# Memory gates stored turned and loaded by transposing DMAs, and a new pacing of the weight sums, in a two-layer decoder trunk

## The chip, the cores and the metric

The kernel runs on one core of one Trainium2 chip. The metric is device time in microseconds (us) of one execution. TensorE (PE in the profile) does the matmuls, VectorE (DVE), ScalarE (ACT) and GpSimd (POOL) the elementwise work. DMAs are issued by SyncE (SP) and by POOL, each through a queue of its own, and share 16 DMA engines.

## The reference

Two layers are computed on a residual stream x of 512 rows by 2048 columns. Each layer projects x with one wide matrix into three groups of heads of 128 columns, each head with a gate path of its own:

```
A) forgetting attention: 6 heads, a log-forget bias, causal
B) sparse attention: 6 heads with rotary; an indexer picks the top 128 keys of each query
C) memory attention: 4 heads into 256 memory rows
y = concat(A, B, C) * silu(gate);  x <- LayerNorm(alpha*x + y @ w_out)
```

What matters here is the gate of group C: a matrix of 512 rows by 4 x 128 columns per layer. The kernel uses it turned, with the 128 columns of a head on the partitions and the 512 rows along them, as the attention output stands when the gate multiplies it.

## The kernel before, in words

**Products.** Every float32 operand is split into a high part that the matmul takes exactly (ACT writes it, `whi`, `xh`) and the rest (DVE writes it, `wlo`, `xl`); a product is three matmuls. A 512-column matmul follows the one before it by about 0.227 us. The weights stream from DRAM in chunks (`raw`, two halves of 128x1024), loaded by SP two chunks ahead (`load_w`, L355); each half is split by ACT and DVE a chunk and a half ahead of its matmuls (`split_w`, L421).

**Stages of a layer.** The tag `now` has the stage's name. "kv": the memory's keys and values. "index": the indexer's small products (chunks `small` and `iq`). "values": for six pairs of column blocks, the projections of values, gates, queries and keys, as seven Strassen-like products per pair (P1, P7, P2, Q6, Q4, then in the next stage Q5 and Q3), so that each column block j = 2 x pair or 2 x pair + 1 comes out as four tiles of 128 rows by 512 columns. "heads": the last two products Q5 and Q3 of all six pairs, with the attention of the 16 heads scheduled between their matmuls. "out": the output projection, again by such products, and then the norm and the next layer's operands (`next_x`, L1484), which run into the next layer's "kv".

**Sums of weights.** Some products need the sum of two weight blocks. Half of the pairs' sums are made ahead in DRAM (`weight_sums`, L556): POOL issues a copy of one block into a `sum` block (1 MB), and later a DMA that adds the other block. There are 44 such DMAs a layer. Each is preceded on POOL by `pool_waits` (L539): DVE (in "values" ACT) writes a small tile `mark`, and POOL waits for it with a multiply into `seen`, so that the sum goes out at that place of the program. `paced` (L573) sets how many ticks lie between two of them. In "kv" and "heads" none is issued. A layer's sums are begun at that layer's "index" stage; `all_sums` (L590) waits after layer 0's last one until layer 1 has begun. Layer 0's 44 sums and layer 1's 44 are otherwise alike. For the P7 product of pairs 1 to 5 no sum is made: the second block is loaded (`other`) and DVE adds it to `raw` (`pair_w`, L383).

**The column blocks' way to the heads.** A finished block is stored in DRAM by POOL and loaded again by SP, one head at a time. There are two ways. Blocks in `ROWS` (L98) are stored by rows as float32 (`store_v`, L1335; a Q5 or Q3 result is added to what is stored by an accumulating DMA) and loaded by head with a strided DMA (`load_head`, L1345, issued at L1349). The others are stored as 16-bit halves, rearranged by ACT (`halves`, L1353; `store_turned`, L1360), and loaded turned by a transposing DMA (`load_turned`, L1374, issued at L1378); a Q5 or Q3 result is added by DVE to what Q6 stored, which SP loads ahead of it (`load_base`, L1317, called at the end of the chunk before). Column block 7 holds the gates of the memory's four heads (`MEMG`), column block 11 those of the last four other heads. Both are in `BY_PE` (L97): they go by rows, and TensorE turns them, four transposes of 128x128 per head into a PSUM bank `gt` (`turned`, L706; `gate`, L716). Block 7 is finished in "heads" by pair 3's Q5 and Q3.

**Order.** "heads" and "out" order their steps with flows (`flow`, `advance`): generators that are stepped between matmuls when a clock modelled in the program says that an engine is free. So a step that becomes longer or falls away moves others. Tiles of 128x512 share a pool of 69 slots; a tile can be written when the slot's earlier tile has been read, by an engine or by a DMA. `store_x` (L1465) stores the next layer's residual (`x<-z`) by POOL; its slots are used again by the operands `xf`, `xh`, `xl` of `next_x`.

Of the kernel before, what the change touches and what calls it, by code (L numbers as in the profile page):

```python
# [23 lines left out]
DEPTH = 2  # L24
# [14 lines left out]
PACE = 2  # L39
# [54 lines left out]
MEMQ, MEMG = 5, 7  # L94
QK = {"f": (2, 4), "d": (6, 8)}
VALUES, GATES = (0, 1, 9), (10, 3, 11)
BY_PE = (7, 11)  # L97
ROWS = (*VALUES, *BY_PE)  # L98
IN_DRAM = 1
VAL_FIRST = (("P1", 0), ("P7", 0), ("P1", 1), ("P7", 1), ("P2", 0), ("Q6", 0), ("Q6", 1), ("P2", 1),  # L100
# [35 lines left out]
def stream():  # L136

    wall = all_chunks()
    where = {c: i for i, c in enumerate(wall)}
    out = []  # L140

    def product(kind, l, name, pair, gs=(0, 1)):
        right = PRODUCTS[name][2]
        for g in gs:
            at = lambda step: where[kind, l, 2 * pair + step[1], 2 * step[0] + g]
            if name in GROWN:
                of, step = GROWN[name]
                src = ("grown", (of, at(step)))
            elif kind == "val" and right == "T3" and pair >= IN_DRAM:
                src = ("pair", tuple(at(step) for step in PAIRED[right]))  # L150
            elif isinstance(right, str):
                src = ("sum", (kind, l, right, pair, g))
            else:
                src = ("wall", at(right))
            out.append(({"val": "vs"}.get(kind, kind), l, (name, pair), g, src))

    for i, c in enumerate(wall):
        kind, l, j = c[:3]
        if kind == "out":
            if c == ("out", l, 0, 0):  # L160
                for name, pair in OUT_ORDER:
                    product("out", l, name, pair)
        elif kind == "val":
            if c == ("val", l, 0, 0):
                early = [x for x in wall if x[1] == l and (x[0], x[2]) in HEAD_CHUNKS]
                for order in (VAL_FIRST, VAL_SECOND):
                    for pair in range(PAIRS):
                        for name, g in order:
                            product("val", l, name, pair, (g,))
                        if order is VAL_FIRST:  # L170
                            for _ in range(EARLY_AT[pair]):
                                x = early.pop(0)
                                out.append((*x, ("wall", where[x])))
        elif (kind, j) not in HEAD_CHUNKS:
            out.append((*c, ("wall", i)))
    return out
# [81 lines left out]
def kernel(  # L258
# [26 lines left out]
    def uid(name):  # L285
        count[0] += 1
        return f"{name}_{count[0]}"
# [16 lines left out]
    def bank(name):  # L304
        return psum.tile([P, 512], F32, tag="b", name=uid(name))
# [13 lines left out]
    def split_lo(src, hi, lo):  # L319
        nc.vector.tensor_tensor(lo, src, hi.bitcast(F32), op=ALU.subtract)  # L320
# [10 lines left out]
    chunks = stream()  # L331
# [85 lines left out]
    def last_half(i):  # L417

        return i >= len(chunks) - 4
# [119 lines left out]
    def pool_waits():  # L539

        mark, seen = small("mark", 1), small("seen", 1)
        if now[1] == "values":
            nc.scalar.activation(mark, mhalf, AF.Copy)
        else:
            nc.vector.tensor_copy(mark, mhalf)
        nc.gpsimd.tensor_tensor(seen, mark, mhalf, op=ALU.mult)
# [3 lines left out]
    def block(kind, l, pair, g, step):  # L550
        return wall[where[kind, l, 2 * pair + step[1], 2 * step[0] + g]]

    def add_weights(key, src):
        nc.gpsimd.dma_start(sums[key], src, accum_op=ALU.add, max_dma_last_dim=2 * DM)

    def weight_sums(kind, l, names, pairs, some=(0, 1)):  # L556

        for name in names:
            for n in some:
                step = SUM_STEPS[name][n]  # L560
                for pair in pairs:
                    for g in range(2):
                        key = (kind, l, name, pair, g)
                        src = block(kind, l, pair, g, step)
                        pool_waits()
                        if n:
                            add_weights(key, src)
                        else:
                            sums[key] = dram.tile([P, DM], F32, name=uid("sum"))
                            nc.gpsimd.dma_start(sums[key], src, max_dma_last_dim=2 * DM)  # L570
                        yield

    def paced(gen):  # L573

        n = 0
        for _ in gen:
            n += 1
            while now[1] in ("kv", "heads"):
                yield 1
            yield {"out": 3, "index": 1 + n % 2}.get(now[1], PACE)  # L580

    def value_sums(l):

        for n in range(2):
            yield from weight_sums("val", l, ("T3",), range(IN_DRAM), (n,))
        for pair in range(PAIRS):
            for n in range(2):
                yield from weight_sums("val", l, ("T1",), (pair,), (n,))

    def all_sums():  # L590


        for l in range(DEPTH):
            yield from paced(value_sums(l))
            yield from paced(weight_sums("out", l, ("T3", "T1"), range(2)))
            while l + 1 < DEPTH and now[0] == l:
                yield 1

    crow_d = [dram.tile([H_FOX, SEQ], F32, name=f"crow{l}") for l in range(DEPTH)]
# [11 lines left out]
    now = (0, "index")  # L611
# [51 lines left out]
    def free(n, eng):  # L663
        banks["held"] -= n
        freed.extend([clock.at[eng] + 0.1] * n)
# [22 lines left out]
    def drain(done):  # L688

        start = clock.at["PE"]  # L690
        while not done():
            advance()
            if not done():
                clock.at["PE"] += 0.2
            assert clock.at["PE"] < start + 100
# [17 lines left out]
    def fetch(key, j, c):  # L713
        return (load_head if j in BY_PE else load_turned)(key, j, c)

    def gate(key, of, there, j):  # L716

        if j in BY_PE:
            yield "PE", 1, there
# [8 lines left out]
        nc.vector.scalar_tensor_tensor(t, t, 1.0, g, op0=ALU.add, op1=ALU.mult)  # L728
        if j in BY_PE:
            free(1, "DVE")  # L730
# [31 lines left out]
    def mem_head(l, j):  # L762
# [3 lines left out]
        nc.sync.dma_start(km.bitcast(F32), km_d[l][j])  # L766
        if MEMQ in BY_PE:
            yield "PE", 1, there + 3
# [8 lines left out]
        split_lo(tp, *q)  # L777
        if MEMQ in BY_PE:
            free(1, "DVE")
# [403 lines left out]
    place_out = [0]  # L1183
# [254 lines left out]
    def load_res(l, st, dc):  # L1438
        z[st, dc] = slot("z")
        src = x_in if l == 0 else x1_d  # L1440
        nc.gpsimd.dma_start(z[st, dc], src[st * P:(st + 1) * P, dc * 512:(dc + 1) * 512])
# [169 lines left out]
    def ahead_of(i):  # L1611
        return i < len(chunks) and chunks[i][0] == "vs" and chunks[i][2][0] in ("Q5", "Q3")

    first = {l: min(i for i, c in enumerate(chunks) if c[1] == l) for l in range(DEPTH)}
    for i, (kind, l, j, col, _) in enumerate(chunks):
        late = last_half(i)
        if kind == "out":
            step = OUT_ORDER.index(j)
            name, pair = j
            if step == col == 0:  # L1620
                now, place_out[0] = (l, "out"), 0
            drain(lambda: (PRODUCTS[name][1], 2 * col + 1) in left)
            chain, aname, _, targets = PRODUCTS[name]
            opens = name in ("P1", "P2", "Q6")
            if col == 0:
                if opens:
                    chains[chain, pair] = [bank("z"), bank("z")]
                zs = chains[chain, pair]

                for st, dc in RES_LOADS.get(step, ()):  # L1630
                    load_res(l, st, dc)
                place_out[0] = step
        elif kind == "vs":
            name, pair = j
            aname = PRODUCTS[name][1]
            opens = name in VAL_OPENS
            if col == 0:
                if opens:
                    chains[VAL_CHAIN[name], pair] = [bank("v"), bank("v")]
            elif ahead_of(i + 1) and 2 * chunks[i + 1][2][1] + 1 not in ROWS:  # L1640
                load_base(*chunks[i + 1][2])
            zs = chains[VAL_CHAIN[name], pair]
        elif kind == "mv":
            if col == 0:
                out_ps = {m: bank("v") for m in range(2)}
        else:
            ps = bank("c")
        for h in range(2):
            n = 2 * i + h
# [27 lines left out]
            if kind == "out" and late:  # L1677
# [6 lines left out]
                if len(kept) == 16:  # L1684
# [3 lines left out]
                    for c in (0, 256):  # L1688
                        ps = bank("z")
                        c = slice(c, c + 256)  # L1690
# [21 lines left out]
            elif kind == "mv":  # L1712
                for m in range(2):
                    for nn in range(2):
                        k = 4 * col + 2 * h + nn
                        c = (k % 2) * 256 + m * P
# [3 lines left out]
            elif kind == "mk":  # L1720
                for kk in range(8):
                    k = 8 * h + kk
                    m = memT[k // 2]
                    c = (k % 2) * 256
# [59 lines left out]
        if kind == "mv" and l > 0:  # L1784
            now = (l, "kv")
        if kind == "small":
            now = (l, "index")
# [8 lines left out]
        if kind == "vs":  # L1796
            now = (l, "heads" if name in ("Q5", "Q3") else "values")
# [11 lines left out]
        if kind == "out" and step == col == 0:  # L1809
            now = (l, "out")  # L1810
# [100 lines left out]
```

## Time and profile before

| | us |
|---|---|
| median of 3 runs | 1887.84 |
| the runs | 1887.82 to 1891.09 |
| the profiled execution | 1887.66 |
| its span, first to last instruction | 1885.8 |
| around the span | 1.9 |
| mean granted TensorE clock | 0.995 |

The traced times are us from the span's start. Layer 0 ends and layer 1 begins at about 936; "heads" lies at about 535 to 810 in layer 0 and at about 1475 to 1750 in layer 1. PE's busy time is that of pipelined matmuls, so a full row says that PE was fed, not that it ran at its peak. A wait shows in PE's rows as a pair of brackets, with the time that PE was idle and what released it.

### The profile page before, as it was taken

What the parts mean: (1) busy time and instruction counts of PE and PEld (TensorE: products, weight loads), DVE (VectorE), ACT (ScalarE), POOL (GpSimd) and SP (SyncE); (2) the same over time, 40 slices, a digit from 0 to 9 for tenths busy, and PEclk for the clock granted to TensorE, in tenths of its full rate; (3) what the DMA queues carried; (4) which work ended last, traced back from release to release, by engine and by line L of the source; (5) the groups of instructions that cost most, each with busy time, mean ns of one, the idle gap of its engine ahead of it and who ended that gap; (6) DMA issues with size and microseconds to landing.
All of it is one profiled execution on the core that took longest, in us unless ns stands there. A gap on an engine that the chain in (4) does not pass through costs nothing.

```text
span 1885.8 us, 26424 instructions
## 1 busy us (share of the span) xinstructions
PE 1856.2 (98%) x8994; PEld 1576.5 (84%) x8994; DVE 1608.6 (85%) x2565; ACT 1079.9 (57%) x1752; POOL 410.1 (22%) x587
## 2 busy tenths in 40 slices
PE   9999999999999999999999999999999999999997
PEld 8998888887888888888899978888878888888886
DVE  6789789888789987889898998889787898878898
ACT  5776344444357887555476753454353578875553
POOL 0121222121233211240011221211221343113302
PEclk9999999999999999999999999999999999999999
DMA  9986998897999887986579969977979998879866
GB/s 351 294 239 162 300 303 241 298 273 267 251 244 286 257 220 206 265 210 215 190 256 282 264 173 307 324 235 272 290 266 237 248 299 234 220 215 269 239 215 142
DMA packets 230372, 474.20 MB, mean 251 GB/s; under 512 B 76368, under 2 KB 100944, under 8 KB 229980
## 3 DMA queue, kind: packets, MB, share of 16 engines
q1 hardware_dynamic: 176508, 300.48, 49.3%
q0 software_dynamic: 53152, 170.97, 35.5%
q8 instruction: 71, 1.16, 0.2%
q10 hardware_dynamic: 576, 1.05, 0.2%
q14 instruction: 65, 0.53, 0.1%
HBM read 402.15 MB, written 149.97 MB: 293 GB/s over the span
## 4 chain that ended last, share of the span: by engine, by line
PE 77%; DVE 9%; DMA 7%; ACT 3%; issue 2%; SPq 0%; POOL 0%; DVEq 0%; ACTq 0%; POOLq 0%
PE v L242 38%; PE c L242 17%; PE z L242 14%; DMA other<-in_wall_dram 4%; DVE wlo L242 4%; PE po L242 3%; PE ix L242 1%; PE s L242 1%; DMA grown<-sum 1%; PE pt L242 1%; ACT whi L242 1%; DVE raw L242 1%; DMA raw<-in_wall_dram 1%; DVE acc L242 1%; DVE rope L242 1%
## 5 line engine op out<-in xcount | busy, mean ns | idle before, releaser
L242 ACT ACTIVATE whi<-raw 128x1024 fp32r<-128x1024 f32 (+1 forms) x497 | 521.3, 1056 | 457.4 <-PE v L242 196.4
L242 DVE TENSOR_TENSOR wlo<-raw,whi 128x1024 fp32r<-128x1024 f32 (+1 forms) x497 | 601.7, 1217 | 133.0 <-ACT whi L242 130.5
L242 PE MATMUL v<-whi,vxh 128*128 128x512 f32 x768 | 306.7, 399 | 8.2 <-ACT whi L242 4.7
L242 PE MATMUL v<-wlo,vxh 128*128 128x512 f32 x768 | 302.0, 393 | 5.0 <-DVE wlo L242 5.0
L242 PE MATMUL v<-whi,vxl 128*128 128x512 f32 x768 | 301.4, 392 | 0.0
L242 PE MATMUL v<-whi,xh 128*128 128x512 f32 x576 | 224.4, 390 | 0.0
L242 PE MATMUL v<-wlo,xh 128*128 128x512 f32 x576 | 224.2, 389 | 0.0
L242 PE MATMUL v<-whi,xl 128*128 128x512 f32 x576 | 224.1, 389 | 0.0
L242 PE MATMUL c<-xh,whi 128*128 128x512 f32 (+1 forms) x544 | 197.9, 364 | 0.0
L242 PE MATMUL c<-xh,wlo 128*128 128x512 f32 (+1 forms) x544 | 197.8, 364 | 0.0
L242 PE MATMUL c<-xl,whi 128*128 128x512 f32 (+1 forms) x544 | 197.7, 363 | 0.0
L242 POOL TENSOR_TENSOR seen<-mark,mhalf 128x1 f32<-128x1 f32 x88 | 58.3, 662 | 635.6 <-ACT mark L242 452.6
L242 PEld LDWEIGHTS v<-whi,vxh 128*128 128x128 f32 x768 | 145.1, 189 | 40.2 <-ACT whi L242 7.4
L242 PEld LDWEIGHTS v<-wlo,vxh 128*128 128x128 f32 x768 | 145.3, 189 | 35.5 <-DVE wlo L242 8.5
L242 PEld LDWEIGHTS v<-whi,vxl 128*128 128x128 f32 x768 | 145.1, 189 | 30.8
L242 PE MATMUL z<-wlo,yh 128*128 128x512 f32 (+1 forms) x434 | 167.8, 387 | 2.0 <-DVE wlo L242 2.0
L242 PE MATMUL z<-whi,yh 128*128 128x512 f32 (+1 forms) x434 | 168.6, 389 | 0.0
L242 PE MATMUL z<-whi,yl 128*128 128x512 f32 (+1 forms) x434 | 167.7, 386 | 0.0
L242 PEld LDWEIGHTS v<-wlo,xh 128*128 128x128 f32 x576 | 108.3, 188 | 23.0 <-DVE wlo L242 0.3
L242 PEld LDWEIGHTS v<-whi,xh 128*128 128x128 f32 x576 | 108.4, 188 | 22.6
L242 PEld LDWEIGHTS v<-whi,xl 128*128 128x128 f32 x576 | 108.1, 188 | 22.6
L242 PEld LDWEIGHTS c<-xl,whi 128*128 128x128 f32 x544 | 102.1, 188 | 12.2
(209 smaller groups left out, 3457.9 us busy)
## 6 DMA issues: line engine op xcount, KB each, us to landing
raw<-in_wall_dram SPq DMA_DIRECT2D x331, 512.0 KB, 7.3
sum<-in_wall_dram POOLq DMA_DIRECT2D x88, 1024.0 KB, 10.5
raw<-sum SPq DMA_DIRECT2D x72, 512.0 KB, 7.4
v<-vraw POOLq DMA_DIRECT2D x88, 256.0 KB, 9.2
other<-in_wall_dram SPq DMA_DIRECT2D x80, 256.0 KB, 13.4
vt<-halves POOLq DMA_DIRECT2D x56, 256.0 KB, 9.6
vraw<-v SPq DMA_DIRECT2D x56, 256.0 KB, 5.1
grown<-in_wall_dram POOLq DMA_DIRECT2D x48, 256.0 KB, 8.8
```

The source lines that it names most:

```text
L242: return f(*args, **kw)
```

## The change

Three things are edited.

1. Column block 7 leaves `BY_PE`, and with it `ROWS`. The memory's gates are now stored as rearranged halves and loaded by transposing DMAs. Per layer, the four tiles from Q5 and Q3 are no longer copied by ACT and stored by an accumulating DMA: SP loads four bases ahead, DVE adds, ACT rearranges, POOL stores. The two tiles of Q6's that are the bases were stored by rows before as well. Sixteen transposes on TensorE per layer, with their bank, fall away; ACT's tanh and DVE's next step read the loaded tile.
2. `paced` yields its pause first and then holds the next sum back, no longer in "kv", but in "heads" and, for layer 1's sums, through its own chunks `mk`, `small` and `iq` 0 to 3 (the set `quiet`). The pause is 2 in "out" (3 before) and 2 in "kv"; in "values" it is 2, and for layer 1's sums 3 after every third.
3. `all_sums` begins layer 1's sums in layer 0's "out" stage, from its tenth of 14 steps on (`place_out` 9).

```diff
-BY_PE = (7, 11)
+BY_PE = (11,)
 ROWS = (*VALUES, *BY_PE)
...
-    def paced(gen):
+    at_chunk = [0]
+    quiet = {i for i, c in enumerate(chunks) if c[0] in ("mk", "small") or c[0] == "iq" and c[2] < 4}
+
+    def paced(l, gen):
 
         n = 0
         for _ in gen:
             n += 1
-            while now[1] in ("kv", "heads"):
+            yield {"out": 2, "kv": 2, "index": 1 + n % 2}.get(now[1], PACE + (l and n % 3 == 0))
+            while now[1] == "heads" or l and at_chunk[0] in quiet:
                 yield 1
-            yield {"out": 3, "index": 1 + n % 2}.get(now[1], PACE)
...
         for l in range(DEPTH):
-            yield from paced(value_sums(l))
-            yield from paced(weight_sums("out", l, ("T3", "T1"), range(2)))
-            while l + 1 < DEPTH and now[0] == l:
+            yield from paced(l, value_sums(l))
+            yield from paced(l, weight_sums("out", l, ("T3", "T1"), range(2)))
+            while l + 1 < DEPTH and now[0] == l and (now[1] != "out" or place_out[0] < 9):
                 yield 1
...
     for i, (kind, l, j, col, _) in enumerate(chunks):
         late = last_half(i)
+        at_chunk[0] = i
```

Up to pair 3's results in layer 0's "heads" every engine's order is as before. The first place where it moves is ACT in that stage. Before, ACT copies pair 3's two tiles (`vraw<-v`) for the accumulating store:

```order
L242 ACTIVATE vraw_6740<-v_6587 128x512
L242 ACTIVATE qh_6749<-rope_6713 128x512
L242 ACTIVATE whi_6728<-raw_6695 128x1024
L242 ACTIVATE vraw_6754<-v_6588 128x512
L242 ACTIVATE pr_6608<-pr_6608,rec_6493 128x512
```

After, it rearranges them (`halves`) once DVE has added the bases:

```order
L242 ACTIVATE whi_6737<-raw_6704 128x1024
L242 ACTIVATE qh_6757<-rope_6722 128x512
L242 ACTIVATE halves_6761<-vraw_6424 128x1024
L242 ACTIVATE halves_6763<-vraw_6426 128x1024
L242 ACTIVATE whi_6767<-raw_6735 128x1024
L242 ACTIVATE pr_6613<-pr_6613,rec_6498 128x512
```

The two copies have become two longer rearrangements, and one `whi` stands ahead of them.

The second place is POOL at the end of layer 0, where the norm's four powers (`rs`), the first sum of layer 1 and the residual's stores (`x<-z`) meet. Before:

```order
L242 TENSOR_TENSOR rs_9264<-rs_9264,mhalf 128x1
L242 TENSOR_TENSOR rs_9269<-rs_9269,mhalf 128x1
L242 TENSOR_TENSOR seen_9320<-mark_9319,mhalf 128x1
L242 DMA sum_9323<-in_wall_dram 256x1024
L242 DMA x_183<-z_7691 128x512
```

After (four more sums stand ahead of the first of these rows):

```order
L242 TENSOR_TENSOR seen_9219<-mark_9218,mhalf 128x1
L242 DMA sum_9222<-in_wall_dram 256x1024
L242 TENSOR_TENSOR seen_9271<-mark_9270,mhalf 128x1
L242 DMA sum_9274<-in_wall_dram 256x1024
...
L242 TENSOR_TENSOR rs_9296<-rs_9296,mhalf 128x1
L242 TENSOR_TENSOR seen_9347<-mark_9346,mhalf 128x1
L242 DMA sum_9222<-in_wall_dram 256x1024
L242 TENSOR_TENSOR seen_9396<-mark_9395,mhalf 128x1
L242 DMA sum_9274<-in_wall_dram 256x1024
L242 TENSOR_TENSOR seen_9487<-mark_9486,mhalf 128x1
```

```order
L242 DMA sum_9490<-in_wall_dram 256x1024
L242 TENSOR_TENSOR seen_9587<-mark_9586,mhalf 128x1
L242 DMA sum_9590<-in_wall_dram 256x1024
L242 DMA x_184<-z_7676 128x512
```

Six sums now stand ahead of the powers, and four instead of one between them and the stores. Those four wait for marks that DVE writes between the operands of `next_x`. The last of the marks, and the operand that takes the slot of the first store's tile (its wait is the store's DMA semaphore), stand in DVE's order after the change like this:

```order
L242 TENSOR_TENSOR vl_9583<-v_9305,vh_9582 128x512 [waits Activation_49]
L242 COPY mark_9586<-mhalf 128x1 [waits Pool_49]
L242 TENSOR_TENSOR xl_9599<-xf_9597,xh_9598 128x512 [waits Activation_49]
...
L242 TENSOR_TENSOR xl_9711<-xf_9709,xh_9710 128x512 [waits DVE_49,Activation_49]
L242 TENSOR_TENSOR xl_9722<-xf_9720,xh_9721 128x512 [waits DMASW3_49,Activation_49]
L242 TENSOR_TENSOR z_7672<-z_7672,row_9276 128x512
L242 TENSOR_TENSOR z_7672<-z_7672,row_9278 128x512 [waits DVE_49]
L242 TENSOR_TENSOR wlo_9732<-raw_9671,whi_9731 128x1024 [waits DMAHW1_49,PE_49,Activation_49]
```

The marks are new there; the order of the operands themselves is that of before, where the mark was written ahead of all of them. Nine sums of layer 1 move to this place from later: five from layer 1's "index" stage and four from its pairs, where the sums behind them each move by one or a few chunks.

## The prediction

> **What bounds the kernel now.** I read the page's busy times and its chain first.
>
> ```profile
> PE 1856.2 (98%) x8994; PEld 1576.5 (84%) x8994; DVE 1608.6 (85%) x2565; ACT 1079.9 (57%) x1752; POOL 410.1 (22%) x587
> PE 77%; DVE 9%; DMA 7%; ACT 3%; issue 2%; SPq 0%; POOL 0%; DVEq 0%; ACTq 0%; POOLq 0%
> ```
>
> The kernel is bound by TensorE: it is fed for 98% of the span. So time can go in two ways: fewer PE instructions, or fewer of the places where PE waits. About 1885.8 - 1856.2 = 29.6 us of the span PE stood idle. Next I looked, window by window, for those places; the columns are the window, its length, busy time (and count) of PE, PE's weight loads, DVE, ACT and POOL, then granted clock, share of the 16 DMA engines, GB/s.
>
> ```profile
> 425.00:438.00 13.00, 10.07 (x36) 7.61 (x35) 10.34 (x15) 6.13 (x10) 1.06 (x2) 0.87 0.64 192
> 1325.00:1335.00 10.00, 10.00 (x46) 8.29 (x45) 7.65 (x11) 5.69 (x7) 3.90 (x5) 1.00 1.02 289
> 1355.00:1366.00 11.00, 11.00 (x50) 9.09 (x50) 6.79 (x10) 2.12 (x2) 1.21 (x2) 1.00 1.05 312
> 1364.00:1377.00 13.00, 9.88 (x31) 7.26 (x30) 10.35 (x15) 6.76 (x10) 1.06 (x2) 0.74 0.59 178
> 1371.00:1376.00 5.00, 5.00 (x13) 3.87 (x13) 4.96 (x7) 3.04 (x6) 1.06 (x2) 0.51 0.55 161
> ```
>
> Two windows of 13 us stand out, in the same place of the two layers (429 is in layer 0's "values", 1366 in layer 1's). At the full pace 11.00 us hold 50 matmuls, so 13 us hold 59. The first holds 36 and the second 31: some 23 x 0.22 = 5.1 us and 28 x 0.22 = 6.2 us are lost. In the second not all of it is waiting: from 1371 to 1376 the granted clock is 0.51, with PE never idle. Just before, the DMA engines are full (1.02 and 1.05 of 16). What PE and DVE wait for, the rows and the chain of waits say:
>
> ```profile
> 1366.38 0.39 PE L242 MATMUL v<-whi,vxl 128*128 128x512 f32 x1
> 1369.38 0.80 PE L242 MATMUL v<-whi,vxh 128*128 128x512 f32 x1 [2.62 <-ACT whi L242]
> 1370.68 0.79 PE L242 MATMUL v<-wlo,vxh 128*128 128x512 f32 x1 [0.50 <-DVE wlo L242]
> 1367.41 0.69 DVE L242 TENSOR_TENSOR raw<-raw,other 128x512 f32<-128x512 f32 x1 [0.84 <-DMA other<-in_wall_dram]
> 1348.77 18.62 DMA other<-in_wall_dram
> other<-in_wall_dram SPq DMA_DIRECT2D x80, 256.0 KB, 13.4
> ```
>
> The block `other` landed 18.62 us after its issue, against a median of 13.4. DVE's add, then the splits, then PE came late. Then the clock fell and the matmuls took 0.8 us.
>
> **The change part by part.**
>
> *Transposes.* Sixteen per layer fall away. One of them is listed with 272 ns, but that is latency; what counts is the chain.
>
> ```profile
> L242 PE MATMUL gt<-ident,vraw 128*128 128x128 f32 x64 | 9.0, 272 | 0.0
> 785.28 1.31 PE gt L242 x12
> ```
>
> Twelve in a row hold the chain for 1.31 us, 0.109 each. 32 x 0.109 = 3.5 us, all on the bounding engine. Taken: **-3.5**. If "heads" waits elsewhere, part of it is lost; least 0 gained.
>
> *The memory gates' new way.* What is added beside PE, per layer: four adds on DVE in place of four copies and with four rearrangements on ACT.
>
> ```profile
> L242 DVE TENSOR_TENSOR vraw<-vraw,v 128x512 f32<-128x512 f32 x40 | 26.2, 680 | 0.0
> L242 ACT ACTIVATE halves<-vraw 128x1024 uint16<-128x1024 uint16 x36 | 36.4, 1047 | 5.0 <-DVE vraw L242 4.7 <-ACT whi L242 0.3
> L242 ACT ACTIVATE vraw<-v 128x512 f32<-128x512 f32 x84 | 47.6, 591 | 22.1 <-PE v L242 21.9
> 680.00:760.00 80.00, 79.22 (x418) 67.16 (x418) 63.65 (x121) 64.17 (x138) 9.91 (x13) 1.00 0.81 218
> ```
>
> DVE gets 4 x 0.68 = 2.7 us more, ACT 4 x (1.05 - 0.59) = 1.8 us. In the 80 us where they fall both have some 16 us free and DMA a fifth; PE is idle for only 0.78 us. So they hide there. If that cover is gone they cost at most 2.7 us a layer. SP issues four base loads more per layer and four transposing loads for four strided ones:
>
> ```profile
> L1349 SPq DMA_DIRECT2D vraw<-v x40: 370/442/1317, 563.4 to 1730.2; - x40
> L1378 SPq DMA_TRANSPOSE vraw<-vt x56: 1165/1333/6414, 535.3 to 1663.0; - x56
> DMA to landing us min/median/max: 2.7/5.1/12.2
> DMA to landing us min/median/max: 2.8/4.9/12.1
> ```
>
> The numbers are ns: least, median, most. A transposing issue holds SP for 0.9 us more at the median, so 4 x 0.9 + 4 x 0.44 = 5.4 us a layer of a queue that otherwise loads weights two chunks ahead. Behind it stand the `raw` loads. From issue to landing both kinds are alike (the last two rows: strided, then transposing). Taken: **0**, between -1.5 and +1.5 a layer, since a shifted order in "heads" gives and takes waits of that size.
>
> The Trainium skill, "DMA: Bandwidth & Descriptors", section Specifications, has a rule against this part: a transfer needs pieces of 512 bytes or more for line rate. The halves have rows of 256 bytes, so by the rule the new loads would land later than the strided ones, which have 512-byte pieces. The trace does not agree: 4.9 against 5.1 us. By the rule the term would be above 0 (a price is given among the rivals); by the row it is 0.
>
> *The stall at 1366.* POOL's rows show what filled the DMA engines ahead of it:
>
> ```profile
> 1320.19 0.92 POOL L242 DMA_DIRECT2D sum<-in_wall_dram  x1
> 1331.04 0.98 POOL L242 DMA_DIRECT2D sum<-in_wall_dram  x1
> 1338.34 0.89 POOL L242 DMA_DIRECT2D sum<-in_wall_dram  x1
> 1355.25 0.96 POOL L242 DMA_DIRECT2D sum<-in_wall_dram  x1
> ```
>
> Four sums of 1 MB in 35 us, by the program's order all four adding ones, which read two blocks to write one. After the change the sums' numbers shift by nine. In this burst then stand two adding sums at the places of 1331 and 1338 and one plain copy at that of 1355; the others have moved to before 1315. I take it that `other` then lands near its median: 18.62 - 13.4 = 5.2 us earlier, more than PE's idle 2.62 + 0.50, so the stall goes and the clock with it. Taken: **-5.8**, most of 6.2, because some tenths of the wait are DVE's own queue. Bounds: -6.2 and -1 (if only the plain copy's lighter load counts). What is late next: the `wlo` behind it, for which PE waited 0.50. Layer 0's stall at 429 stays, since its sums do not move.
>
> "TensorE: Matmul & The Clock Gate" of the Trainium skill, Part 1, says that the clock halves only after an idle window of about 3.4 us. Here two idle pieces of 2.62 and 0.50 us were enough for a clock of 0.51 afterwards. By the rule a stall under 3.4 us would cost only itself; by the rows it costs about twice as much, and so I count this one.
>
> *A new wait where the layers meet.* Four sums now stand on POOL between the powers and the residual's stores, the last behind a mark that DVE writes after `vl`.
>
> ```profile
> 936.98 2.26 POOL L242 TENSOR_TENSOR rs<-rs,mhalf 128x1 f32<-128x1 f32 x4 [93.89 <-DVE rs L242]
> 944.36 0.43 POOL L242 TENSOR_TENSOR seen<-mark,mhalf 128x1 f32<-128x1 f32 x1 [5.11 <-DVE mark L242]
> 944.73 0.66 POOL L242 DMA_DIRECT2D sum<-in_wall_dram  x1
> 945.38 2.44 POOL L242 DMA_DIRECT2D x<-z  x4
> DMA to landing us min/median/max: 9.3/10.2/11.4
> 962.16 1.28 DVE L242 TENSOR_TENSOR vl<-v,vh 128x512 fp32r<-128x512 f32 x2
> 970.56 0.69 DVE L242 TENSOR_TENSOR xl<-xf,xh 128x512 fp32r<-128x512 f32 x1 [0.64 <-ACT xh L242]
> 972.50 1.22 DVE L242 TENSOR_TENSOR wlo<-raw,whi 128x1024 fp32r<-128x1024 f32 x1
> 976.73 0.28 PE L242 MATMUL c<-memh,wlo 128*128 128x256 f32 x1
> 980.29 2.35 DVE L242 TENSOR_TENSOR wlo<-raw,whi 128x1024 fp32r<-128x1024 f32 x2
> 982.49 0.28 PE L242 MATMUL c<-memh,wlo 128*128 128x256 f32 x1
> 936.00:966.00 30.00, 30.00 (x180) 26.40 (x179) 29.86 (x57) 24.03 (x33) 5.73 (x10) 1.00 0.60 207
> ```
>
> The last mark comes at 962.2 + 1.3 = 963.4; with `seen` and the sum's issue (0.43 + 0.66) the first store goes at 964.5 instead of 945.4. Behind one sum it landed 9.3 to 11.4 us after its issue, so now between 973.8 and 975.9; with the longest landing of the rows above, 12.2, at 976.7. Its slot is that of the operand `xl` of 970.56, and behind that stand z and `wlo` on DVE. This `wlo` was ready at 973.7 and PE used it at 976.7, 3.0 us to spare; the first of the two of 980.29 was ready at about 981.5 for 982.5, 1.0 to spare. DVE has no room to catch up (29.86 of 30 us busy up to 966). So DVE is 3.2 to 6.1 us late, less a spare of 1.0 to 3.0: 0.2 to 5.1 us on PE. Taken **+2.1**: the landing's median, 964.5 + 10.2 = 974.7, is 4.1 late, less 2.0, the middle of the spare. Its ends are 0 (it lands by 971.6) and 5.1. The four powers also come up to 1.1 us later behind a sum: **+0.4**, between 0 and 1.1.
>
> *The rest.* Layer 0's end gets six sums more:
>
> ```profile
> 885.00:935.00 50.00, 50.00 (x222) 41.44 (x221) 41.59 (x60) 25.55 (x30) 0.00 (x0) 1.00 0.65 210
> ```
>
> A third of the DMA engines is free, and PE never waits. A sum each 9 us at, by my estimate from 1 MB moved two to three times at 312 GB/s, near 3.5 us of all engines brings this to 1.0: full, not over. Taken 0, at most +2. In "index" five marks fewer leave DVE a little freer; taken 0.
>
> Sum: -3.5 + 0 - 5.8 + 2.1 + 0.4 = -6.8. From the profiled execution's 1887.66 (0.2 us below the median, 1.9 of it outside the span, which no edit touches) this is **1880.9**.
>
> **The rivals.**
>
> *The stall stays or only moves* (no change). For it: layer 0's stall of 5.1 us is at the same place with the same loads of `other`; a burst of `other`s and `raw`s may fill the engines without the sums. Against it: the sums' numbers differ, and with four adding ones it was the longer of the two. Then -3.5 + 2.1 + 0.4, with up to -1 for the lighter copy, makes 1885.7 to 1886.7.
>
> *The wait where the layers meet is hidden* (faster). If the store lands by 971.6, in 7.1 us, `xl` is late by no more than the spare and the term of 2.1 falls away: 1878.8. For it: four sums with the last a plain copy; against: before, it was 9.3 us behind one sum.
>
> *SP is held by the transposing loads* (slower). Mechanism: in "heads" SP waits in order for a stored tile, and a long transposing issue then delays the weights behind it. By the rows the longest issue took 6.41 against 0.44 us. Two such per layer are 11.9 us; less a spare of 2 us, the middle of the two above, +9.9 a layer: 1880.9 + 19.8 = 1901. Slower begins at 1891.6, 10.7 above the forecast, so it decides from 5.4 + 2 = 7.4 us of holding a layer. Against it: 56 such issues happened in "heads" with a median of 1.33 us, and PE's idle time there is 1%.
>
> *The gates land late* (slower). If the new loads landed as late as the longest of their kind, 12.1 - 5.1 = 7 us later, the gate's tanh and the head's last product would wait. The flows put other matmuls there; one uncovered head a layer makes 2 x 7 = 14: 1895. Against it: the median of 4.9. It is what the rule on small pieces, named above, would do here.
>
> **How the numbers follow.** My forecast (stall gone, wait where the layers meet up to 5.1): 0.50, 1878.5 to 1884. Hidden wait: 0.18. Stall stays or moves: 0.22. Gates late: 0.03. SP held: 0.07. The range runs from the hidden wait with the ends of the stall and of "heads" (1878.8 - 0.4 - 2.4 = 1876.0) to the staying stall with +1.3 in "heads" (1888.0), and leaves out the two slower rivals and fringes: **1876 to 1888**. A measurement of this kernel tells apart about 0.2%, 3.8 us: faster is below 1884.0, slower above 1891.6. The forecast and the hidden wait are nearly all faster, and a tenth of the staying stall (with the wait hidden and a gain in "heads"): 0.70. Same: the rest of that rival, 0.20. Slower: 0.10.
>
> **What would show it.** Right: PE has 32 matmuls fewer; no `other` waits between 1355 and 1372 and the clock is 1.00 there, while 425 to 438 still shows 36 matmuls in 13 us; POOL issues the x stores at about 965; DVE has an idle piece of some 2 to 6 us before an `xl` near 971, released by a DMA `x<-z`. Wrong: a window with a clock near 0.5 anywhere in layer 1's "values", a PE wait in "heads" released by `tanh` or `halves`, or SP's longest transposing issue above 7 us with `raw` late behind it.

## The result and the profile after

| | us |
|---|---|
| before, median of 6 runs | 1887.83 |
| after, median of 6 runs (1894.77 to 1908.43) | 1904.06 |
| ratio after to before | 1.0088 (1.007 to 1.0106) |
| after, the profiled execution | 1903.38 |
| its span | 1901.6 |

The change makes the kernel slower by 16 us. The forecast was 1880.9, with a range of 1876 to 1888.

The page of the changed kernel, its busy times and its chain:

```profile
PE 1858.6 (98%) x8962; PEld 1574.5 (83%) x8962; DVE 1615.7 (85%) x2577; ACT 1082.3 (57%) x1748; POOL 416.0 (22%) x587
PE 66%; DMA 10%; DVE 10%; issue 9%; ACT 3%; POOL 1%; SPq 0%; DVEq 0%; ACTq 0%; POOLq 0%
```

PE has 32 matmuls fewer, as it should, but its share of the chain fell from 77% to 66%. Windows of the changed kernel show where (length, busy time and count of PE, PE's loads, DVE, ACT, POOL, then clock, DMA share, GB/s):

```profile
425.00:438.00 13.00, 12.20 (x54) 9.61 (x53) 12.52 (x17) 8.04 (x12) 1.05 (x4) 1.00 0.75 212
760.00:780.00 20.00, 16.00 (x63) 11.55 (x63) 10.16 (x14) 7.40 (x12) 1.20 (x2) 0.91 1.03 220
975.00:995.00 20.00, 14.31 (x102) 13.90 (x101) 9.66 (x14) 10.11 (x15) 3.30 (x7) 0.83 0.76 267
1355.00:1390.00 35.00, 35.00 (x156) 29.00 (x155) 31.90 (x43) 15.31 (x20) 5.17 (x8) 1.00 0.76 239
```

The stall that stood at 1366 is gone, as forecast: 156 matmuls in 35 us, clock 1.00. In layer 0's window from 425 to 438, where the program is that of before, 54 matmuls stand instead of 36, so that stall varies from one execution to the next. The new losses are in two places.

**Where "heads" goes over into "out".** Of 20 us from 760 on, PE is idle for four, and the clock falls. I added up how much longer each matmul took to start after the one before than the median of its kind. From 560 to 840 these excesses make 6.1 us before and 19.6 after; from 1480 to 1800, the same stage of layer 1, 6.1 and some 14. SP's queue and the chain at that place, after:

```profile
744.12 6.05 SPq L1381 DMA_TRANSPOSE vraw<-vt  x1
751.85 10.46 SPq L1381 DMA_TRANSPOSE vraw<-vt  x1
762.41 1.91 SPq L373 DMA_DIRECT2D raw<-in_wall_dram  x2
762.41 12.55 DMA raw<-in_wall_dram
775.07 1.06 ACT whi L242
776.18 0.66 PE L242 MATMUL z<-whi,yh 128*128 128x512 f32 x1 [2.12 <-ACT whi L242]
```

The gate loads of the third and fourth memory head hold SP for 6.05 and 10.46 us. The weights behind the second are issued at 762.41, where before five were issued from 750.19 on; they land 12.55 us later and PE waits. The transposing loads' rows, and the DMA part of the window from 750 to 770, first after, then before (q0 is POOL's queue, q1 SP's: packets, MB, and the time that the packets took as a share of the 16 engines' time):

```profile
L1381 SPq DMA_TRANSPOSE vraw<-vt x64: 1165/1374/10465, 531.1 to 1704.4; - x64
DMA to landing us min/median/max: 3.0/5.4/22.0
DMA packets 3107, 3.52 MB, mean 176 GB/s; under 512 B 2094, under 2 KB 2094, under 8 KB 3106
q0 software_dynamic: 778, 1.89, 60.6%
q1 hardware_dynamic: 2328, 1.62, 59.0%
```

```profile
DMA packets 3076, 6.43 MB, mean 322 GB/s; under 512 B 291, under 2 KB 1315, under 8 KB 3075
q1 hardware_dynamic: 2321, 4.57, 63.5%
q0 software_dynamic: 754, 1.84, 38.8%
```

Two transposing loads are in flight there. The longest landed 22.0 us after its issue. All queues together moved 3.52 MB in 20 us instead of 6.43, with the DMA engines' share at 1.20 instead of 1.03. POOL's queue moved as much as before, but its packets took 60.6% of the engines' time instead of 38.8%; SP's queue, with the weights and the gates, moved about a third of what it did before.

**Where the layers meet.** POOL's queue, the chain and DVE, after:

```profile
958.30 5.91 POOL L242 TENSOR_TENSOR seen<-mark,mhalf 128x1 f32<-128x1 f32 x1 [4.57 <-DVE mark L242]
964.78 5.51 POOL L242 TENSOR_TENSOR seen<-mark,mhalf 128x1 f32<-128x1 f32 x1
971.58 2.91 POOL L242 TENSOR_TENSOR seen<-mark,mhalf 128x1 f32<-128x1 f32 x1 [0.74 <-DVE mark L242]
975.01 2.20 POOL L242 DMA_DIRECT2D x<-z  x4
975.01 12.20 DMA x<-z
977.75 0.69 DVE L242 TENSOR_TENSOR xl<-xf,xh 128x512 fp32r<-128x512 f32 x1 [3.32 <-DMA vm<-vh]
987.30 0.69 DVE L242 TENSOR_TENSOR xl<-xf,xh 128x512 fp32r<-128x512 f32 x1 [6.62 <-DMA x<-z]
990.51 0.58 PE L242 MATMUL c<-memh,wlo 128*128 128x256 f32 x1 [3.67 <-DVE wlo L242]
```

This is the wait that the prediction named, at the operand that it named: DVE is idle for 6.62 us until the store has landed. It is larger than forecast. All stands 7.9 us later here, so the forecast's issue at 964.5 and landing at 974.7 are 972.4 and 982.6. The store left at 975.0, because `seen`, a multiply of 128x1, took 2.9 to 5.9 us three times over; and it landed in 12.20 us, not 10.2. An operand ahead of it had already waited 3.32 us for another store, one of the memory's values (`vm<-vh`). SP issues that one at the same place in both kernels; it landed 2.3 us after its issue before and 10.1 after, where the DMA engines' share is 1.07 (970 to 980) and not 0.54 (960 to 970 before). PE waited 3.67 us there, 2.02 just before, and then ran at half clock. The excess is 8.1 us in the 40 us from 960 on.

### The profile page after: what moved, and what is told of

It reads as the page before. It is cut to its first block, busy times and chain, and to the rows that moved or that the text cites. A ratio compares the mean times of both kernels' runs of the same rounds, so it can differ in the third digit from the quotient of the medians.

```text
span 1901.6 us, 26384 instructions
## 1 busy us (share of the span) xinstructions
PE 1858.6 (98%) x8962; PEld 1574.5 (83%) x8962; DVE 1615.7 (85%) x2577; ACT 1082.3 (57%) x1748; POOL 416.0 (22%) x587
## 4 chain that ended last, share of the span: by engine, by line
PE 66%; DMA 10%; DVE 10%; issue 9%; ACT 3%; POOL 1%; SPq 0%; DVEq 0%; ACTq 0%; POOLq 0%
PE v L242 33%; PE c L242 17%; PE z L242 9%; DMA other<-in_wall_dram 5%; DVE wlo L242 4%; PE po L242 2%; DMA raw<-in_wall_dram 2%; PE ix L242 2%; DMA grown<-sum 1%; ACT whi L242 1%; PE s L242 1%; DMA v<-vraw 1%; PE pt L242 1%; DVE rope L242 1%; DVE raw L242 1%
## 5 line engine op out<-in xcount | busy, mean ns | idle before, releaser
L242 POOL TENSOR_TENSOR seen<-mark,mhalf 128x1 f32<-128x1 f32 x88 | 66.0, 750 | 695.2 <-ACT mark L242 457.8
L242 PEld LDWEIGHTS c<-xl,whi 128*128 128x128 f32 x544 | 102.1, 188 | 12.2
```

Source lines behind the costliest of these rows:

```text
L242: return f(*args, **kw)
```

## The experiments

Theory A says that the loss in "heads" and "out" comes with the gates' new way and the rest with the pacing; theory B that the denser sums make it all. Four kernels separate the parts. Below, ratios are against runs of before on the same chip.

**e1, the gates alone.**

```diff
-BY_PE = (7, 11)
+BY_PE = (11,)
```

> Only the memory gates' new way; the pacing is that of before. Theory A, the transposing gate loads hold SP where "heads" goes over into "out": the losses of PE there stay as in the changed kernel (19.6 us between 560 and 840 and 14.3 between 1480 and 1800, against 6.1 and 6.1 before), less 3.5 for the transposes, so 1887.8 + 21.7 - 3.5 = 1906, with SP rows of two transposing loads over 5 us in layer 0. Theory B, the denser sums in "out" fill the DMA engines there and the gates are harmless: 1884.

1895.77, ratio 1.0055 (1.0035 to 1.0075). That is between the two theories, 10 us under A's 1906: the excess at the end of "heads" is some 14 us over both layers in this run's profile, not 22, and of the two loads there one held SP for 8.86 us, the other for 2.39. **e2, the pacing alone** (the change's other hunks, with `BY_PE = (7, 11)`):

> Only the new pacing and the early start of layer 1's sums; the memory gates go by rows and TensorE. Theory A: the stall where the layers meet stays (8 us), the one at 1366 is gone (6 us), nothing is lost in "heads": 1887.8 + 8 - 6 = 1890. Theory B: the loss of 21.7 us in "heads" comes with this part: 1911.

1891.51, ratio 1.0031 (1.0015 to 1.0046). The two parts cost 10 and 6 us and make up the 16; theory B falls. Of the two parts, the excess at the end of "heads" is in e1 alone, the one where the layers meet (9.8 us) in e2 alone. In e2 the chain goes there not through the residual's store but through another of the memory's values, `vm<-vl`, which landed 14.64 us after its issue. The stall at 1366 is in e1 and not in e2. Rows of e1, then of e2:

```profile
1364.00:1381.00 17.00, 13.84 (x49) 10.54 (x48) 12.89 (x16) 8.14 (x11) 1.06 (x2) 0.80 0.69 197
```

```profile
970.00:990.00 20.00, 13.65 (x89) 13.15 (x88) 11.78 (x17) 10.19 (x15) 1.34 (x3) 0.75 0.72 239
1355.00:1390.00 35.00, 35.00 (x156) 29.00 (x155) 32.31 (x43) 15.32 (x20) 3.37 (x6) 1.00 0.73 241
```

**e3 and e4, no sums in "kv".** e3 is the changed kernel with this edit, e4 the pacing alone with it:

```diff
-            while now[1] == "heads" or l and at_chunk[0] in quiet:
+            while now[1] in ("kv", "heads") or l and at_chunk[0] in quiet:
```

> The changed kernel, but no sums in "kv", as before: the residual's stores are no longer behind four marks on POOL. If the stores' wait is what costs 8 us where the layers meet, that stall goes and this run takes 1904 - 8 = 1896. The rival, that the stall there is the DMA engines' (six sums just before), leaves it at 1904.

> Only the new pacing, without sums in "kv". Theory A: neither stall of the changed kernel is left and the one at 1366 is gone: 1882, faster than before. Theory B: 1903.

1923.03, ratio 1.02 (1.0181 to 1.0219), and 1914.37, ratio 1.0155 (1.0138 to 1.0172). The stall where the layers meet went, from 8.1 us of excess to under 0.1. But these runs are 27 and 32 us above what I expected, lost in a new place: without the four sums in "kv", and with the new pauses, layer 1's sums run on to the start of its "heads". Windows of e4 there, then POOL's last sum, SP, and the load of `ck` that PE's scores wait for:

```profile
1460.00:1480.00 20.00, 20.00 (x90) 16.57 (x89) 19.51 (x33) 12.18 (x16) 8.78 (x12) 1.00 1.12 281
1480.00:1500.00 20.00, 17.97 (x80) 14.55 (x78) 7.28 (x12) 2.92 (x4) 0.11 (x1) 1.00 1.25 102
1500.00:1520.00 20.00, 0.80 (x1) 0.29 (x1) 3.47 (x5) 4.19 (x6) 9.02 (x17) 0.51 1.07 175
1479.24 0.87 POOL L242 DMA_DIRECT2D sum<-in_wall_dram  x1
1466.72 18.65 SPq L1381 DMA_TRANSPOSE vraw<-vt  x2
1485.41 24.08 DMA ck<-crow
```

The same picture as at 750, in a stage where the memory gates play no part: transposing loads (of queries and keys) meet full DMA engines, the rate falls to 102 GB/s with the engines' share at 1.25, and SP is held for 18.65 us by two loads; the second of them took 15.30 us with nothing to wait for. In before the last sum is issued at 1448.05, some 18 us ahead of those loads, and the chain does not leave PE there.

So theory A was split: A1, the transposing as such; A2, the small pieces of 256 bytes; A3, a bad place in the queue, where SP waits for a slot (the view of SP's waits after the change puts 9.0 us of the load at 751.85 down to PE's `ptm`).

**e5 and e6, plain loads in the same place.** e1, with the memory gates' loads as plain DMAs of the same bytes (e6 with `"(p a) c -> p (a c)"`, 2 KB pieces). All engines' order is that of e1.

```diff
-        nc.sync.dma_start_transpose(t.bitcast(U16).rearrange("p (a r) -> p a r", a=1), vt_d[j][c])
+        if j == MEMG:
+            nc.sync.dma_start(t.bitcast(U16).rearrange("p (a c) -> p a c", a=8),
+                              vt_d[j][c].rearrange("(a p) c -> p a c", a=8))
+        else:
+            nc.sync.dma_start_transpose(t.bitcast(U16).rearrange("p (a r) -> p a r", a=1), vt_d[j][c])
```

> The kernel with only the gates' new way, its order unchanged, but the memory gates' 4 loads per layer are plain DMAs of the same 256 KB in pieces of 256 bytes, not transposing ones (ACT leaves the halves in place, and the gates' values are not the reference's). Theory A1, the transposing itself fills the DMA engines and holds SP: the losses at the end of "heads" go, 1895.8 - 12 = 1884. Theory A2, the small pieces do: it stays at 1896. Theory A3, the loads only stand in a bad place and wait there for a slot: it stays at 1896.

> As the run before, with pieces of 2 KB (the values again not the reference's). Theories A1 and A2: 1884. Theory A3, the wait for a slot: 1896.

1884.33, ratio 0.9988 (0.9975 to 1.0001), and 1885.01, ratio 0.9992 (0.9979 to 1.0005). By the ratios they give back some 12 us of what e1 lost. A2 and A3 fall: neither the size of the pieces nor the place in the queue makes the loss, but that the loads transpose. The window of e5 and its gate loads:

```profile
750.00:770.00 20.00, 20.00 (x106) 16.87 (x105) 16.85 (x31) 15.41 (x33) 4.01 (x6) 1.00 1.07 332
746.75 0.85 SPq L1379 DMA_DIRECT2D vraw<-vt  x1
754.47 1.26 SPq L1379 DMA_DIRECT2D vraw<-vt  x1
```

332 GB/s, PE never idle, and 0.85 and 1.26 us on SP for the two loads in the same places. Nor was `ptm` what the load at 751.85 waited for. TensorE's order is the same in all these kernels, so its `sm` can date the slot; a row of SP's waits in e6, then one of the chain after the change:

```profile
SPq L1379 <- PE sm L242: 2.8, 1, 2.8
```

```profile
746.83 1.43 PE sm L242 x12
```

In e6 the same load left at 753.01, as soon as that `sm` was done. After the change it was done at 748.3, ahead of the load, so the slot was free.

The Trainium skill, "DMA: Bandwidth & Descriptors", Specifications, asks for 512 bytes or more per transfer. The two runs' times do not differ between pieces of 256 bytes and 2 KB. Their packets do, and there the trace agrees: summed from the traces, the packets of the third and fourth head's loads took 2.5 us of all 16 engines in e5 and some 1.4 in e6.

**e7, the transposing loads in a quieter place.** e1, with the gates of the third and fourth memory head loaded together with their queries:

```diff
-        yield "PE", 0, 0.0, lambda: kept_by(MEMQ)
+        yield "PE", 0, 0.0, lambda: kept_by(MEMQ) and (j < 2 or kept_by(MEMG))
         there = fetch(("mq", j), MEMQ, j)
+        if j > 1:
+            gate_there = fetch(("mg", j), MEMG, j)
...
-        there = fetch(("mg", j), MEMG, j)
+        there = gate_there if j > 1 else fetch(("mg", j), MEMG, j)
```

> The kernel with only the gates' new way, but the gates of the third and fourth memory head are loaded with their queries, some 10 to 20 us earlier, where the DMA engines are three quarters busy. Theories A1 and A2 (traffic): the transposing loads land in under 6 us, the loss at the end of "heads" falls by most of 12 us: 1885 to 1888. Theory A3: depends on the new slots; 1896 if the wait for a slot stays.

1884.39, ratio 0.998 (0.9969 to 0.9992). The same loads, still transposing, some 20 us earlier, cost 11 us less by the medians (14 by the ratios); they landed 3.4 to 3.9 us after their issue. SP's rows, and the window that was jammed:

```profile
725.88 2.50 SPq L1380 DMA_TRANSPOSE vraw<-vt  x2
731.80 3.35 SPq L1380 DMA_TRANSPOSE vraw<-vt  x2
750.00:770.00 20.00, 20.00 (x104) 16.94 (x103) 16.18 (x29) 15.35 (x33) 4.87 (x7) 1.00 1.05 335
```

**e8, the stores by SP.** e2, with the four stores of `next_x` issued by `nc.sync`:

```diff
-                    store_x(st, 1)
+                    store_x(st, 1, nc.sync)
```

> The kernel with only the new pacing, with the four residual stores of next_x issued by SP and not by POOL behind the marks. If their late landing is the 9.8 us lost where the layers meet: 1891.5 - 9.8 = 1882. The rival, that the full DMA engines make that loss: 1891.

1887.81, ratio 1.0003 (0.9993 to 1.0014), against e2's 1.0031: about 5 of the 9.8 us come back; by the excesses 9.8 became 4.3. That lies between the two values expected. What is late next are the stores of the memory's values. DVE's row in e8, then the windows from 960 to 970 of e8 and of before:

```profile
976.50 0.69 DVE L242 TENSOR_TENSOR xl<-xf,xh 128x512 fp32r<-128x512 f32 x1 [6.29 <-DMA vm<-vh]
960.00:970.00 10.00, 10.00 (x88) 10.00 (x87) 9.74 (x16) 9.84 (x16) 7.62 (x4) 1.00 1.06 306
```

```profile
960.00:970.00 10.00, 10.00 (x88) 10.00 (x87) 9.33 (x14) 9.81 (x16) 0.00 (x0) 1.00 0.54 161
```

SP issued `vm<-vh` at about 960 in both; it landed 15.4 us later in e8 and 2.3 before. So the four sums in "kv" cost in two ways: they hold back the residual's stores on POOL, and they fill the DMA engines when the values' stores go out. The first is shown by e8 and e9, both together by e3; the second alone is read from these rows, and no run tests it by itself.

**e9, both mends in the changed kernel** (e7's and e8's edits).

> The changed kernel with both mends: the third and fourth memory head's gates loaded early, and the four residual stores of next_x by SP. If the transposing loads in full DMA engines and the late stores are the two causes, it gives back 11 and 4 of the 16 us: 1904 - 15 = 1889 or a little under. If the parts also hinder each other, it stays over 1895.

1883.83, ratio 0.9991 (0.9981 to 1.0002) where the changed kernel has 1.0088: some 18 us come back by the ratios, where 15 were expected, and it is level with before.

**e10 and e11, what makes the stalls at 429 and 1366.** The forecast put them down to adding sums. e10 is e7 with the early start of layer 1's sums alone; e11 is e7 with the pacing of before, and the sums for "out" in another order:

```diff
-            yield from paced(weight_sums("out", l, ("T3", "T1"), range(2)))
+            for name in ("T3", "T1"):
+                for pair in range(2):
+                    yield from paced(weight_sums("out", l, (name,), (pair,)))
```

> The gates' new way with the early loads (1884.4 alone) and, of the new pacing, only the early start: four of layer 1's sums go out in layer 0's "out" stage, none more in "kv" than before. The sums' numbers in the burst before 1366 then shift by four, from four adding ones to four copies. If adding sums make that stall, it goes: 1884.4 - 5.5 = 1879, and nothing is lost where the layers meet. If any four sums make it, it stays: 1884.

> The gates' new way with the early loads and the pacing of before, but the sums for "out" are made pair by pair: two copies, two adding ones, and so on, in both layers. In the bursts before 429 and 1366 then stand two copies and two adding sums, not four adding ones. If the adding ones make the two stalls, both shrink: 1884.4 - 5 to - 10, 1874 to 1879. If the number of sums makes them: 1884.

1878.95, ratio 0.9964 (0.995 to 0.9977), and 1874.52, ratio 0.9943 (0.9931 to 0.9955). In e10 the stall of layer 1 is gone and that of layer 0, whose sums do not move, is there; in e11 both are gone. By the ratios e10 is 3 us under e7, which the intervals do not tell apart, and e11 is 7. Windows of e10, then of e11:

```profile
425.00:438.00 13.00, 10.09 (x32) 7.47 (x31) 9.69 (x14) 5.61 (x9) 1.06 (x2) 0.75 0.61 189
1350.00:1375.00 25.00, 25.00 (x112) 20.68 (x111) 22.78 (x29) 12.30 (x17) 3.91 (x6) 1.00 0.69 207
```

```profile
425.00:438.00 13.00, 13.00 (x59) 10.77 (x58) 12.39 (x16) 8.20 (x13) 2.51 (x4) 1.00 0.58 189
1340.00:1370.00 30.00, 30.00 (x134) 24.83 (x133) 27.37 (x36) 14.26 (x19) 4.95 (x7) 1.00 0.81 255
```

As many sums as before, at the same marks, with two adding ones in the burst instead of four, leave no stall. The excess from 420 to 445, which differs from one execution to the next, is 1.2 to 6.3 us in the twelve profiles with four adding sums there and 0.0 in the two with mixed ones (e11 and e12). e11 beats both kernels: before by 12 us, of which e7 had 2.6, and the changed one by the ratios 0.9943 against 1.0088.

**e12, all gates turned.** e11 with `BY_PE = ()`: no gate is transposed on TensorE.

> The best kernel so far (1874.5) with column block 11 stored turned too: no transposes are left on TensorE for gates (3.5 us less), and the last four heads' gates come by transposing loads, three of them in a row where the DMA engines are 0.76 to 0.85 busy and the output projection's weights are loaded behind them on SP. If transposing loads cost what the place makes them cost, three in a row there hold SP and the weights as in the changed kernel: +5 a layer, 1874.5 - 3.5 + 10 = 1881, with transposing issues of 3 us or more. If only full DMA engines (1.0 and more) make them dear: 1871.

1894.98, ratio 1.0041 (1.0026 to 1.0057). 18 us slower than e11 by the ratios (20 by the medians), with 3.5 us of PE's work removed: the new loads cost more than twice the 10 us expected of the dearer case. Rows of SP and the window behind them:

```profile
766.82 5.17 SPq L1382 DMA_TRANSPOSE vraw<-vt  x3
786.90 2.70 SPq L1382 DMA_TRANSPOSE vraw<-vt  x1
780.00:800.00 20.00, 20.00 (x104) 17.35 (x103) 14.83 (x32) 7.85 (x18) 9.36 (x12) 1.00 1.03 145
```

The issues are short here, and the three in a row, with a share of 0.67 from 764 to 774, landed 3.3 to 5.9 us after their issue. The single one at 786.90 landed after 14.8, and in its window the price is again the rate, 145 GB/s at full engines (e11: 251 at 0.97). Behind it `grown<-sum` lands 18.62 us after its issue, and PE waits 10.13 us at 802.

## Why the prediction was wrong, point by point

- *Transposes, -3.5:* not contradicted. PE has 32 matmuls fewer, and e7, which keeps the new way and pays nothing for its loads' place, is 2.6 us under before by the medians.
- *The memory gates' new way, taken 0, between -1.5 and +1.5 a layer:* **this is the step that failed.** e1's 10.1 us and the 3.5 saved make it +13.6, 6.8 a layer. About 1 us a layer is the longer work on DVE and ACT, which e5 and e7 still show as waits of PE near 680 and 720; the rest, some 5.7, is two transposing loads in full DMA engines. I took "from issue to landing both kinds are alike" from medians over the whole stage. The new loads went out at 744 and 752, and a window of before from 750 to 770 would have shown full engines (1.03), 322 GB/s and five loads of weights in SP's queue.
- *The rival "SP is held":* its mechanism took place, with issues of 6.05 and 10.46 us, at a chance of 0.07. It was priced by the issue alone, at 9.9 us a layer; the measured 5.7 lies under that. The sign named for it, an issue above 7 us with `raw` late behind it, came. What it missed is that the full engines make the issue long, and that the loads also make other transfers take longer.
- *The rule on small pieces:* named as what could speak against the change, it pointed at the right loads for a reason that e5 against e6 rules out here.
- *The stall at 1366, -5.8:* right. It is gone in every kernel with shifted or mixed sums, and the cause, adding sums in the burst, is shown by e10 and e11. The shift itself is of one sum at that place, not of nine, by the order of the DMAs in the two kernels; it is enough to put the two adding sums and the copy where the prediction has them. *Layer 0's stall stays:* it does in e2 and e10; in the execution profiled after the change it was mostly absent.
- *The wait where the layers meet, +2.1 (0 to 5.1):* right in place, and in mechanism for a part; too small. It measured 8.1 us after the change and 9.8 in e2. Left out was that the four sums also fill the DMA engines, so that the values' stores land late; e8, with the residual's stores out of the marks' way, keeps 4.3 us, which the trace puts down to that. Mis-sized were the way from the mark to the store (`seen` up to 5.9 us), the landing (12.2) and, left out as well, the half clock behind a wait of 2.02 and 3.67 us, which I had charged at 1366 but not here.
- *The clock:* waits of less than 3.4 us do cost more than themselves. After the change PE waited 2.12 and 0.60 us at 776, and the clock of the next stretch was 0.50; it was 0.50 from 776.5 to 777.4 already, before the second wait was over. In e1 two waits of 0.90 and 0.81 us at 430 were followed by a full clock:

```profile
777.00:782.00 5.00, 4.56 (x11) 3.60 (x12) 5.00 (x8) 4.81 (x8) 1.48 (x3) 0.50 0.19 56
```

```profile
425.00:438.00 13.00, 11.13 (x47) 8.35 (x46) 11.91 (x15) 8.15 (x12) 1.06 (x2) 1.00 0.73 187
```

"TensorE: Matmul & The Clock Gate" of the Trainium skill, Part 1, has a free-running window of some 3.4 us that must be idle. The trace agrees with the window: in the records of the granted clock the half-speed stretches last 3.41 us (before, at 433.8), 6.83 (after, at 776.4) or 10.24 (e2, at 979.9). The first row falls after less idle time than that; a window mostly idle seems to be enough, which no run here tests by itself.

- *The powers, +0.4 (0 to 1.1):* right in size. Against the matmuls ahead of them POOL's powers came 0.4 us later (7.9 instead of 7.5), TensorE's matmuls behind them 0.2.
- *The sums:* "1 MB moved two to three times at 312 GB/s" makes 6.7 to 10 us and not 3.5. The share at layer 0's end came to 0.87 after the change (885 to 935), and PE does not wait there. The range takes 2.4 us for the end of "heads" where the term itself allows 1.5 a layer.

## What to carry to other kernels

In these runs a DMA that transposes was cheap only where the DMA engines had room: price it by what else is in flight when it runs, and look at GB/s beside the busy share, since engines that are full at half the rate were its mark here. Move it ahead rather than give it up: 20 us made 11 us here. And when copies and adding DMAs come in runs, mix them; as many bytes at the same pace, in another order, took away two stalls here.

## What the runs showed of the hardware

DMA engines that were full (share 1.03 to 1.25) moved 102, 145 and 176 GB/s in three places while transposing loads were in flight; in the windows of the second and third, kernels without such loads there show 251 to 335. From 750 to 770 after the change, the packets of 256 bytes, which only the two gate loads have there, took 7.3 us of all 16 engines, summed from the trace. Plain loads of the same bytes in the same pieces took 2.5 in e5, and one transposing load at 721, where the engines had room, took 1.2 and landed 3.0 us after its issue. The rest of what the window lost is that the other packets took longer too. Why a transposing load differs so much between the two places stays open.

POOL's multiply of 128x1 took 0.19 us at 936 and 944 and 5.9 us at 958, where DVE and ACT had hardly any idle time (6.00 and 5.91 of 6 us). The three long ones, 5.91, 5.51 and 2.91 us, took the same in e2. Each began while DVE ran operations on two tiles of SBUF back to back (`xl`, `vx`, `wlo`), and each ended 0.05 us after the last of such a run, at 964.16, 970.24 and 974.44; beside a run on one tile, `z<-z,mv,rs` at 952, it took 0.36. So it seems to wait out such a run; no edit tests it.
